# A two-layer model on one core: where bias weights are loaded, how means over partitions are taken, and the shape of the gated scores

## The chip, the cores and the metric

The kernel runs on one core of one Trainium2 chip. A core has TensorE (matrix products, called PE in the profile, with PEld for its weight loads), VectorE (DVE), ScalarE (ACT), GpSimd (POOL) and SyncE (SP), from whose queue all DMAs of this kernel are issued. The metric is the device time of one execution in microseconds.

## The reference, cut to what matters

The sequence has 2048 tokens of width 1024, everything is f32. Layer A is gated linear attention (4 heads, keys of 128, values of 256, chunks of 64 tokens), layer B is stick-breaking attention (16 heads of 64). Each is wrapped in an RMS norm, a modulation by a condition vector and a residual.

```
rms_norm(x) = x * rsqrt(mean(x*x over the width) + eps) * gain
shift, scale, gate = split(silu(c) @ w_ada + b_ada, 3)
h = rms_norm(x) * (1 + scale) + shift
# layer A, per head and chunk of 64 tokens, b = cumsum(log_sigmoid(gk)/16) in the chunk
scores = tril((q * exp(b)) @ (k * exp(-b)).T)
o = scores @ v + (q * exp(b)) @ state
state = exp(b_last) * state + (k * exp(b_last - b)).T @ v
x = x + gate * ((rms_norm(o) * silu(g)) @ w_out)
# layer B: k, v from hk = rms_norm(x)*(1+kv_scale)+kv_shift; q, g from h
# out = rms_norm(x + gate * (stick_breaking(q, k, v) * silu(g)) @ w_out, final_gain)
```

## The kernel before, in words

Activations lie transposed: the width is on the 128 partitions in 8 tiles (`KT`), and 512 tokens (`TG`) are the free dimension, so there are four groups of tokens (`NG`). A mean over the width is therefore a mean over partitions. `rstd` (L205) takes it on TensorE: the sum of squares over the 8 tiles, a [128x512] f32 tile, is multiplied by a 128x128 matrix of 1/1024 (`mean_d`) or 1/256 (`mean_v`), which leaves the mean on every partition; ScalarE and VectorE make the inverse root of it.

Most products are in three terms: a value is `hi`, rounded to fp32r by ScalarE, and `lo`, what is left, by VectorE (`split`, L221); `mm3` (L135) multiplies hi by hi, hi by lo and lo by hi. A product of plain f32 operands is in the trace as two matmul instructions.

`start` (L300) makes the first group's input: it loads x, starts the rows of the condition's weights (`ada_rows`, 16 tiles wa_l of 512 KB which VectorE multiplies into an accumulator aa_l), normalises x on GpSimd (L315), sums the accumulator over partitions (`ada_sum`, 16 matmul instructions for each half), and makes xn = x*a + b on VectorE, ScalarE and GpSimd (`scaled`, L327), then hi and lo of it. In this part the order of TensorE, ScalarE, VectorE and SP is that of the code.

`layer0` (L690) runs layer A group by group: value, key and query projections head by head (`qkv`), the gate (`gate`), the attention of a head (`gla`), the output gate and the output projection. `play` steps one main generator and beside it side generators with a delay and a stride, and so fixes TensorE's order; one yield of `mm3` is three matmuls. The order on the other engines is made by a planner from priorities (the order of the code, moved by `urgent` and `relaxed`) and its own estimate of times; at run time each engine takes its instructions in that fixed order. `gla` takes the scores of two chunks (128 keys by 128 queries) in one product (L466) and overwrites the corner where queries of the second chunk meet keys of the first by a 64 by 64 product with other key weights, `kn` (L467). After a head's output `po` come the squares (`ss_o`), five yields, and `rstd`. `normed_out` (L568) does the norm of a finished group (`ss_y`, `r_y`, x1n) as a side generator while the next group runs.

`bias_sums` (L655) runs in the third and fourth group: it loads the weights of layer B once (16 halves of 512 KB for each of two matrices, tiles wb), multiplies them by the shift on VectorE, and sums over partitions with two transposes and a reduction. Its tiles come from the pool `wraw` (3 buffers), as do the raw weights of every load (`load_half`, L104, DMA issued at L106) and later rows of the condition's weights. The pool `wsp` (10 buffers) holds hi and lo of two weight blocks, 4 buffers each; `m2` (22 buffers) holds [128x512] tiles.

Layer B (`layer1`) computes projections, scores, a scan and products with the values; its last stage `final` ends with an `rstd` per group and two half groups at the end.

Of the kernel before, what the change touches and what calls it, by code (L numbers as in the profile page):

```python
# [16 lines left out]
P = 128  # L17
# [17 lines left out]
def yoco_kernel(ctx: ExitStack, tc: tile.TileContext, I: dict, O: dict):  # L35
# [29 lines left out]
    def bank(pool, name):  # L65
# [7 lines left out]
    nc.gpsimd.memset(ident, 1.0)  # L73
    nc.gpsimd.affine_select(ident, ident, pattern=[[-1, P]], compare_op=ALU.is_equal,
                            fill=0.0, base=0, channel_multiplier=1)
    mean_d = cpool.tile([P, P], F32, tag="mean_d", name="mean_d")
    nc.vector.memset(mean_d, 1.0 / D)
    mean_v = cpool.tile([P, P], F32, tag="mean_v", name="mean_v")
    nc.vector.memset(mean_v, 1.0 / GV)
    ones = cpool.tile([P, 1], F32, tag="ones", name="ones")  # L80
    nc.vector.memset(ones, 1.0)
    epsc = cpool.tile([P, 1], F32, tag="epsc", name="epsc")
# [122 lines left out]
    def rstd(name, sq, mean, n=TG):  # L205


        ms = bank(po, f"ms_{name}")[:, 0:n]
        sq = sq if isinstance(sq, list) else [sq]
        for i, x in enumerate(sq):  # L210
            nc.tensor.matmul(ms, mean, x, start=i == 0, stop=i == len(sq) - 1)
        r = t2(f"r_{name}")[:, 0:n]
        q = t2(f"rq_{name}")[:, 0:n]
        nc.scalar.activation(r, ms, AF.Ln, bias=epsc)
        nc.scalar.activation(r, r, AF.Exp, scale=-0.5)
        nc.scalar.activation(q, r, AF.Square)
        nc.vector.scalar_tensor_tensor(q, ms, epsc, q, op0=ALU.add, op1=ALU.mult)
        nc.vector.scalar_tensor_tensor(r, q, -3.0, r, op0=ALU.add, op1=ALU.mult)
        return r
# [56 lines left out]

    def normed_in(T):

        r = rstd(f"x{T.g}", T.ss, mean_d)
        yield  # L280
        yield
        for i in range(4):
            xs = load_x(T.g, i, "xx")
            for j in range(2):
                modulate(T, 2 * i + j, xs[j], r)
                yield
# [13 lines left out]
    def start():  # L300

        T = start_group(0)
        w = I["w_ada"][0]
        rows = [ada_rows("l0", w, j, act) for j in range(2)]
        xs, sq = [], []
        for i in range(4):
            xs += load_x(0, i)
            for kt in (2 * i, 2 * i + 1):
                sq.append(t2(f"sq_x0_{kt}"))
                nc.scalar.activation(sq[kt], xs[kt], AF.Square)  # L310
        for _ in range(6):
            next(rows[0])
        r = rstd("x0", sq, mean_d)
        for kt in range(KT):
            nc.gpsimd.tensor_tensor(xs[kt], xs[kt], r, op=ALU.mult)  # L315
        accs = [result(g) for g in rows]
        gate_weights()
        ahead.append(next(blocks))
        cond = new_cond("l0", 2)
        pc = bank(po, "pc_l0")  # L320
        for j in range(2):
            ada_sum(pc[:, 8 * j:8 * j + 8], accs[j])
        nc.vector.tensor_tensor(cond, pc[:, 0:16], b_ada[:, 0:16], op=ALU.add)
        a, b = mods["l0m"] = modulation("l0", norm_gain[:, 0:8], cond)
        xn = [t2(f"xn_0_{kt}") for kt in range(KT)]

        def scaled(kt):  # L327
            s, t = a[:, kt:kt + 1], b[:, kt:kt + 1]
            if kt % 2 == 0 and kt:
                nc.scalar.activation(xn[kt], xs[kt], AF.Identity, bias=t, scale=s)  # L330
            else:
                eng = nc.vector if kt < 1 else nc.gpsimd
                eng.tensor_scalar(xn[kt], xs[kt], s, t, op0=ALU.mult, op1=ALU.add)

        scaled(0)
        for kt in range(KT):
            if kt + 1 < KT:
                scaled(kt + 1)
            h = new_h(0, kt)
            T.hs.append(split(h[:, 0], h[:, 1], xn[kt]))  # L340
        return T


# [38 lines left out]
    def gate(T, h):  # L382


        n = f"{T.g}_{h}"
        u = bank(po, f"u_{n}")
        nc.tensor.matmul(u, gk2[:, h * P:(h + 1) * P], T.lr[0:96], start=True, stop=True)
        bg = b_gk[:, h:h + 1]
        gk = t2(f"gk_{n}")
        e = t2(f"e_{n}")  # L390
        nc.vector.tensor_scalar(gk, u, bg, 0.0, op0=ALU.add, op1=ALU.min)
        nc.scalar.activation(e, u, AF.Abs, bias=bg)
        nc.scalar.activation(e, e, AF.Exp, scale=-1.0)
        nc.scalar.activation(e, e, AF.Ln, bias=1.0)
        nc.vector.tensor_tensor(gk, gk, e, op=ALU.subtract)
        b64 = e
        b128 = t2(f"b128_{n}")
        b64c = b64.rearrange("p (c t) -> p c t", t=64)
        b128c = b128.rearrange("p (c t) -> p c t", t=128)
        nc.vector.tensor_tensor_scan(b64, masks[:, 0], gk, 0.0, ALU.mult, ALU.add)  # L400
        nc.vector.tensor_tensor_scan(b128, masks[:, 1], gk, 0.0, ALU.mult, ALU.add)

        bl = m2.tile([P, 8], F32, tag="bl", name=f"bl_{n}", bufs=2)
        nc.vector.tensor_scalar(bl[:, 0:4], b128c[:, :, 127], 1.0 / GN, None, op0=ALU.mult)
        nc.vector.tensor_scalar(bl[:, 4:8], b64c[:, 0::2, 63], 1.0 / GN, None, op0=ALU.mult)
        G = Piece()
        G.ke, G.kf, G.kn, G.qe, G.qf = gk, t2(f"kf_{n}"), t2(f"kn_{n}"), b64, b128
        nc.scalar.activation(G.ke, b64, AF.Exp, scale=-1.0 / GN)
        for s in range(4):
            nc.scalar.activation(G.kf[:, s * P:(s + 1) * P], b128[:, s * P:(s + 1) * P], AF.Exp,  # L410
                                 bias=bl[:, s:s + 1], scale=-1.0 / GN)
            nc.scalar.activation(G.kn[:, s * 64:(s + 1) * 64], b64c[:, 2 * s, :], AF.Exp,
                                 bias=bl[:, 4 + s:5 + s], scale=-1.0 / GN)
        nc.scalar.activation(G.qe, b64, AF.Exp, scale=1.0 / GN)
        nc.scalar.activation(G.qf, b128, AF.Exp, scale=1.0 / GN)
        G.dec = m2.tile([P, 4], F32, tag="dec", name=f"dec_{n}", bufs=3)
        nc.scalar.activation(G.dec, bl[:, 0:4], AF.Exp)
        T.G[h] = G

    def qkv(T, h):  # L420
# [26 lines left out]
        yield from mm3(pk, wkq, 0, T.hs)  # L447
        with urgent():
            nc.vector.tensor_tensor(G.ke, pk, G.ke, op=ALU.mult)
            kn = G.kn[:, 0:256].rearrange("p (c t) -> p c t", t=64)  # L450
            nc.vector.tensor_tensor(kn, pk.rearrange("p (c t) -> p c t", t=64)[:, 0::2, :], kn, op=ALU.mult)
            nc.vector.tensor_tensor(G.kf, pk, G.kf, op=ALU.mult)
        pq = bank(pl, f"pq_{n}")
        yield from mm3(pq, wkq, 1, T.hs)
# [4 lines left out]
    def gla(T, h):  # L459
# [3 lines left out]
        psc = bank(pw, f"psc_{n}")  # L463
        for s in range(4):
            c0 = s * P
            nc.tensor.matmul(psc[:, c0:c0 + P], G.ke[:, c0:c0 + P], G.qe[:, c0:c0 + P], start=True, stop=True)  # L466
            nc.tensor.matmul(psc[0:64, c0 + 64:c0 + P], G.kn[:, s * 64:(s + 1) * 64],  # L467
                             G.qe[:, c0 + 64:c0 + P], start=True, stop=True)
            yield
        sc = t2(f"sc_{n}")  # L470
        with urgent():
# [42 lines left out]

        with urgent():
            ss = result(sumsq_steps(f"o{n}", pos))
        for _ in range(5):
            yield
        r = rstd(f"o{n}", ss, mean_v)
        on = t4(f"on_{n}", [P, 2, TG])  # L520
        for v2 in range(2):
            nc.vector.scalar_tensor_tensor(on[:, v2], pos[v2], o_gain[:, v2:v2 + 1], r,
# [45 lines left out]
    def normed_out(T):  # L568

        g = T.g  # L570
        ss = yield from sumsq_steps(f"y{g}", T.x1, 100)
        for _ in range(10):
            yield
        r = rstd(f"y{g}", ss, mean_d)
        for f in range(KT):
            nc.vector.tensor_tensor(T.x1[f], T.x1[f], r, op=ALU.mult)
            xn = tact(f"x1n_{g}_{f}")
            split(xn[:, 0], xn[:, 1], T.x1[f])
            nc.sync.dma_start(xn_d[g][:, f], xn.bitcast(F32))
            yield  # L580
# [74 lines left out]
    def bias_sums(i):  # L655
# [10 lines left out]
            nc.vector.tensor_reduce(biases[:, at:at + 2], pb.rearrange("p (j t) -> p j t", j=2),  # L666
                                    axis=mybir.AxisListType.X, op=ALU.add)

        before = None
        for p in range(SBP):  # L670
            acc = t2(f"bs_{i}_{p}")[:, 0:2 * P]
            for hf in range(2):
                raw = wraw.tile([P, 4, 256], F32, tag="wraw", name=f"wb_{i}_{p}_{hf}")
                nc.sync.dma_start(raw, I[which][p][:, 4 * hf:4 * hf + 4, :])
                for j in range(4):
                    kt = 4 * hf + j
                    s = b[:, kt:kt + 1]
                    with relaxed(200):
                        if kt == 0:
                            nc.vector.tensor_scalar(acc, raw[:, j], s, None, op0=ALU.mult)  # L680
                        else:
                            nc.vector.scalar_tensor_tensor(acc, raw[:, j], s, acc, op0=ALU.mult, op1=ALU.add)
                yield
            if before:
                total(*before)
            before = p, acc
        yield
        total(*before)

# [224 lines left out]
    def final(g, t0=0, n=TG):  # L914
# [8 lines left out]
        for fp in range(4):  # L923
# [9 lines left out]
            for j in range(2):  # L933
# [3 lines left out]
                                                   op0=ALU.mult, op1=ALU.add)  # L937
                x2s.append(x2[:, j])
                ss.add(x2[:, j])
        r = rstd(f"f{name}", ss.acc, mean_d, n)  # L940
        for f in range(KT):
            with relaxed(400):
                nc.vector.scalar_tensor_tensor(x2s[f], x2s[f], final_gain[:, f:f + 1], r,
# [182 lines left out]
```

## Time and profile before

| | us |
|---|---|
| median of 3 runs (lowest to highest) | 2676.28 (2675.8 to 2679.9) |
| the profiled execution, whole | 2677.76 |
| its span in the trace | 2676.1 |
| TensorE busy in the span | 2595.5 (97%) |
| VectorE busy | 2127.7 (80%) |
| ScalarE busy | 1519.0 (57%) |
| GpSimd busy | 171.4 (6%) |
| mean granted TensorE clock, as a share of full speed | 0.985 |

The trace is of one execution. A busy time counts instructions, and matmuls are pipelined, so the chain of waits gives the step from one matmul to the next better than the length of one instruction does. The span runs from the first to the last instruction; the 1.66 us between it and the whole lie outside the trace.

### The profile page before, as it was taken

The page shows a single profiled execution, that of the slowest core. Times are in us where ns is not written, and L with a number is a line of the kernel's source. Part 1 is how long each engine was busy: PE and PEld are TensorE (multiplying, and loading weights), DVE is VectorE, ACT ScalarE, POOL GpSimd, SP SyncE. Part 2 cuts the span into 40 slices and gives each one's busy share as a digit, 9 for nine tenths or more (in the row PEclk, how much of TensorE's full clock was granted, in tenths as well). Part 3 has the DMA queues.
Part 4 walks back from the last instruction along what each step waited for, and adds up shares of the span by engine and source line. Part 5 has one row for each costly group of instructions (what it writes and reads, how often), then busy time and mean ns, then how long its engine had stood idle before and what let it go on. Part 6 is the DMA issues. An engine that isn't in the chain of part 4 may idle for free.

```text
span 2676.1 us, 38236 instructions
## 1 busy us (share of the span) xinstructions
PE 2595.5 (97%) x14008; PEld 2184.6 (82%) x14008; DVE 2127.7 (80%) x2933; ACT 1519.0 (57%) x2677; POOL 171.4 (6%) x358
## 2 busy tenths in 40 slices
PE   5999999989998999999999999999999999999998
PEld 4888888878787887888888888888888888887887
DVE  7647667687867657987988978989889889889866
ACT  4746755564666435655655655556556556566644
POOL 3000000000000001001001010010010010010000
PEclk7999999989999999999999999999999999999999
DMA  6326345455744375424323333424233243413464
GB/s 248 118 72 212 126 163 184 157 197 173 252 157 160 133 245 207 168 75 150 110 103 123 120 133 104 153 79 170 83 138 119 77 148 111 146 64 123 151 213 144
DMA packets 121292, 388.70 MB, mean 145 GB/s; under 512 B 14384, under 2 KB 18608, under 8 KB 121104
## 3 DMA queue, kind: packets, MB, share of 16 engines
q1 hardware_dynamic: 121104, 386.25, 41.8%
q8 instruction: 111, 1.82, 0.3%
q14 instruction: 77, 0.63, 0.1%
HBM read 328.52 MB, written 40.89 MB: 138 GB/s over the span
## 4 chain that ended last, share of the span: by engine, by line
PE 82%; DVE 8%; ACT 5%; DMA 4%; issue 1%; SPq 0%; DVEq 0%; ACTq 0%
PE pt L862 9%; PE o L880 5%; PE z L846 5%; PE o L879 5%; PE z L845 5%; PE lq L142 2%; PE lk L142 2%; PE lg L142 2%; PE lk L143 2%; PE lk L144 2%; PE lg L143 2%; PE lq L143 2%; PE lg L144 2%; PE lq L144 2%; PE pf L142 2%; PE pf L143 2%
## 5 line engine op out<-in xcount | busy, mean ns | idle before, releaser
L865 ACT ACTIVATE sh<-pt 128x512 fp32r<-128x512 f32 (+3 forms) x640 | 340.4, 532 | 526.5 <-PE pt L862 516.6
L866 DVE SCALAR_TENSOR_TENSOR sl<-pt,sh 128x512 fp32r<-128x512 f32 (+3 forms) x640 | 384.9, 602 | 147.2 <-ACT sh L865 141.6
L854 DVE TENSOR_TENSOR_SCAN S<-S,S 128x512 f32<-128x512 f32 x384 | 490.1, 1276 | 9.0 <-ACT S L849 7.3
L862 PE MATMUL pt<-ident,S 128*128 128x128 f32 x2176 | 343.7, 273 | 7.2 <-DVE sl L866 7.2
L849 ACT ACTIVATE S<-z 128x512 f32<-128x512 f32 (+3 forms) x640 | 339.3, 530 | 14.8 <-PE o L880 5.8
L862 PEld LDWEIGHTS pt<-ident,S 128*128 128x128 f32 x2176 | 270.8, 140 | 81.6 <-DVE sl L866 13.1
L845 PE MATMUL z<-k,q 128*128 128x512 f32 (+3 forms) x640 | 283.3, 443 | 0.0
L880 PE MATMUL o<-sl,v 128*128 128x512 f32 (+3 forms) x640 | 233.7, 365 | 0.0
L846 PE MATMUL z<-k,ql 128*128 128x512 f32 (+3 forms) x640 | 233.3, 365 | 0.0
L879 PE MATMUL o<-sh,v 128*128 128x512 f32 (+3 forms) x640 | 230.2, 360 | 0.0
L854 DVE TENSOR_TENSOR_SCAN S<-S 128x128 f32<-128x128 f32 (+3 forms) x256 | 209.5, 821 | 17.3 <-POOL S L851 14.0
L851 POOL TENSOR_SCALAR_AFFINE_SELECT S<-S 128x128 f32<-128x128 f32 x256 | 86.7, 339 | 1228.3 <-ACT S L849 1228.3
L436 PE MATMUL pv<-wh_v,h 128*128 128x256 f32 x512 | 157.7, 308 | 0.0
L437 PE MATMUL pv<-wl_v,h 128*128 128x256 f32 x512 | 146.8, 287 | 0.0
L438 PE MATMUL pv<-wh_v,h 128*128 128x256 f32 x512 | 146.7, 286 | 0.0
L879 PEld LDWEIGHTS o<-sh,v 128*128 128x128 f32 x640 | 120.3, 188 | 28.4
L880 PEld LDWEIGHTS o<-sl,v 128*128 128x128 f32 x640 | 120.5, 188 | 26.5
L845 PEld LDWEIGHTS z<-k,q 128*128 128x128 f32 x640 | 121.7, 190 | 6.1
L846 PEld LDWEIGHTS z<-k,ql 128*128 128x128 f32 x640 | 123.2, 193 | 0.2
L142 PE MATMUL pg<-h,wh_g 128*128 128x512 f32 x256 | 112.7, 440 | 0.0
L142 PE MATMUL lv<-xb,wh_w_kv 128*128 128x512 f32 x256 | 104.6, 408 | 4.5 <-DVE g L823 3.1
L436 PEld LDWEIGHTS pv<-wh_v,h 128*128 128x128 f32 x512 | 99.9, 195 | 7.0 <-issue 2.8
(266 smaller groups left out, 6353.4 us busy)
## 6 DMA issues: line engine op xcount, KB each, us to landing
xb<-xn SPq DMA_DIRECT2D x256, 512.0 KB, 5.5
wa_l<-in_w_ada_dram SPq DMA_DIRECT2D x40, 512.0 KB, 5.0
wr_f<-in_w_out_dram SPq DMA_DIRECT2D x40, 512.0 KB, 4.2
x<-in_x_dram SPq DMA_DIRECT2D x32, 512.0 KB, 7.1
wr_v<-in_w_v_dram SPq DMA_DIRECT2D x32, 512.0 KB, 4.5
wr_kq<-in_w_kq_dram SPq DMA_DIRECT2D x32, 512.0 KB, 4.0
wr_g<-in_w_g_dram SPq DMA_DIRECT2D x32, 512.0 KB, 4.0
wr_out<-in_w_out_dram SPq DMA_DIRECT2D x32, 512.0 KB, 3.8
```

The costliest lines, as they stand in the source:

```text
L142: nc.tensor.matmul(out, hi, x[kt][0], start=first and i == 0, stop=False)
L143: nc.tensor.matmul(out, hi, x[kt][1], start=False, stop=False)
L436: nc.tensor.matmul(o, xh, hi, start=i == 0, stop=False)
L845: nc.tensor.matmul(z, L.q[:, h, tcol], k[:, h, 0:w], start=True, stop=False)
L846: nc.tensor.matmul(z, L.ql[h][:, tcol], k[:, h, 0:w], start=False, stop=True)
L849: nc.scalar.activation(s, z, AF.Sigmoid, scale=-SCALE_B)
L854: nc.vector.tensor_tensor_scan(s[:, ::-1], s[:, ::-1], s[:, ::-1], 1.0 if diag else self.before.S[tb][:, 0:1], ALU.mult, ALU.min)
L862: nc.tensor.transpose(pt[:, tb * P:(tb + 1) * P], self.S[tb][:, sb * P:(sb + 1) * P], ident)
L865: nc.scalar.activation(hi, pt[:, t0 * P:], AF.Copy, bias=-1.0)
L866: nc.vector.scalar_tensor_tensor(lo, pt[:, t0 * P:], -1.0, hi.bitcast(F32), op0=ALU.add, op1=ALU.subtract)
L879: nc.tensor.matmul(o, v, hi, start=self.diag and sb == 0, stop=False)
L880: nc.tensor.matmul(o, v, lo, start=False, stop=self.c == 0 and sb == 3)
```

## The change

Five edits. The matrices of 1/1024 and 1/256 are also kept in fp32r (`mean_r`), and `rstd` of a single tile splits that tile in hi and lo on ScalarE and VectorE and makes two fp32r products in place of one f32 product; in `gla` it comes seven yields after the squares and in `normed_out` 16 yields in all groups but the last (10 there). `start` leaves GpSimd out: VectorE makes x*a*r in one instruction, ScalarE adds b and rounds to hi, VectorE makes lo. The gated scores are two products of 128 keys by 64 queries; `kn` has 128 keys, those of the second chunk with the weights of `ke`, so `gate` makes one more exponential and `qkv` multiplies a whole tile. `bias_sums` takes its tiles from `wsp` and issues the next load right after the multiplications of the one before; the sums over partitions of one accumulator come one step after its last multiplication (three before).

```
-    mean_d = cpool.tile([P, P], F32, tag="mean_d", name="mean_d")
+    mean_d = t2("mean_d")[:, 0:P]
     nc.vector.memset(mean_d, 1.0 / D)
-    mean_v = cpool.tile([P, P], F32, tag="mean_v", name="mean_v")
-    nc.vector.memset(mean_v, 1.0 / GV)
+    mean_r = {}
+    for name, n in ("d", D), ("v", GV):
+        mean_r[name] = cpool.tile([P, P], F32R, tag=f"mean_{name}", name=f"mean_r{name}")
+        nc.scalar.activation(mean_r[name], mean_d, AF.Copy, scale=float(D / n))
...
 def rstd(name, sq, mean, n=TG):
-        sq = sq if isinstance(sq, list) else [sq]
-        for i, x in enumerate(sq):
-            nc.tensor.matmul(ms, mean, x, start=i == 0, stop=i == len(sq) - 1)
+        if isinstance(sq, list):
+            for i, x in enumerate(sq):
+                nc.tensor.matmul(ms, mean_d, x, start=i == 0, stop=i == len(sq) - 1)
+        else:
+            hi = t2(f"sh_{name}", F32R)[:, 0:n]
+            lo = t2(f"sl_{name}", F32R)[:, 0:n]
+            with urgent():
+                split(hi, lo, sq)
+            for i, x in enumerate((hi, lo)):
+                nc.tensor.matmul(ms, mean_r[mean], x, start=i == 0, stop=i == 1)
...
 def start():
-        for kt in range(KT):
-            nc.gpsimd.tensor_tensor(xs[kt], xs[kt], r, op=ALU.mult)
-        accs = [result(g) for g in rows]
-        gate_weights()
-        ahead.append(next(blocks))
-        cond = new_cond("l0", 2)
-        pc = bank(po, "pc_l0")
+        cond, pcs = new_cond("l0", 2), []
         for j in range(2):
-            ada_sum(pc[:, 8 * j:8 * j + 8], accs[j])
-        nc.vector.tensor_tensor(cond, pc[:, 0:16], b_ada[:, 0:16], op=ALU.add)
+            acc = result(rows[j])
+            if j:
+                gate_weights()
+                ahead.append(next(blocks))
+            pcs.append(bank(po, f"pc_l0_{j}"))
+            ada_sum(pcs[j], acc)
+        for j in range(2):
+            cols = slice(8 * j, 8 * j + 8)
+            nc.vector.tensor_tensor(cond[:, cols], pcs[j][:, 0:8], b_ada[:, cols], op=ALU.add)
         a, b = mods["l0m"] = modulation("l0", norm_gain[:, 0:8], cond)
         def scaled(kt):
-            s, t = a[:, kt:kt + 1], b[:, kt:kt + 1]
-            if kt % 2 == 0 and kt:
-                nc.scalar.activation(xn[kt], xs[kt], AF.Identity, bias=t, scale=s)
-            else:
-                eng = nc.vector if kt < 1 else nc.gpsimd
-                eng.tensor_scalar(xn[kt], xs[kt], s, t, op0=ALU.mult, op1=ALU.add)
+            h = new_h(0, kt)
+            xn = t2(f"xn_0_{kt}")
+            nc.vector.scalar_tensor_tensor(xn, xs[kt], a[:, kt:kt + 1], r, op0=ALU.mult, op1=ALU.mult)
+            nc.scalar.activation(h[:, 0], xn, AF.Identity, bias=b[:, kt:kt + 1])
+            return h, xn
...
+            h, xn = ready[kt]
+            nc.vector.scalar_tensor_tensor(h[:, 1], xn, b[:, kt:kt + 1], h[:, 0].bitcast(F32),
+                                           op0=ALU.add, op1=ALU.subtract)
...
 def gate(T, h):
-            nc.scalar.activation(G.kn[:, s * 64:(s + 1) * 64], b64c[:, 2 * s, :], AF.Exp,
+            nc.scalar.activation(G.kn[:, s * P:s * P + 64], b64c[:, 2 * s, :], AF.Exp,
                                  bias=bl[:, 4 + s:5 + s], scale=-1.0 / GN)
+        nc.scalar.activation(G.kn.rearrange("p (c t) -> p c t", t=P)[:, :, 64:], b64c[:, 1::2, :], AF.Exp,
+                             scale=-1.0 / GN)
...
 def qkv(T, h):
-            kn = G.kn[:, 0:256].rearrange("p (c t) -> p c t", t=64)
-            nc.vector.tensor_tensor(kn, pk.rearrange("p (c t) -> p c t", t=64)[:, 0::2, :], kn, op=ALU.mult)
+            nc.vector.tensor_tensor(G.kn, pk, G.kn, op=ALU.mult)
...
 def gla(T, h):
-            nc.tensor.matmul(psc[:, c0:c0 + P], G.ke[:, c0:c0 + P], G.qe[:, c0:c0 + P], start=True, stop=True)
-            nc.tensor.matmul(psc[0:64, c0 + 64:c0 + P], G.kn[:, s * 64:(s + 1) * 64],
-                             G.qe[:, c0 + 64:c0 + P], start=True, stop=True)
+            for at, k in (c0, G.ke), (c0 + 64, G.kn):
+                nc.tensor.matmul(psc[:, at:at + 64], k[:, c0:c0 + P], G.qe[:, at:at + 64], start=True, stop=True)
...
-        for _ in range(5):
+        for _ in range(7):
             yield
-        r = rstd(f"o{n}", ss, mean_v)
+        r = rstd(f"o{n}", ss, "v")
...
 def normed_out(T):
-        for _ in range(10):
-            yield
-        r = rstd(f"y{g}", ss, mean_d)
+        yield from pause(16 if g + 1 < NG else 10)
+        r = rstd(f"y{g}", ss, "d")
...
 def bias_sums(i):
+        def load(p, hf):
+            raw = wsp.tile([P, 4, 256], F32R, tag="wsp", name=f"wb_{i}_{p}_{hf}").bitcast(F32)
+            nc.sync.dma_start(raw, I[which][p][:, 4 * hf:4 * hf + 4, :])
+            return raw
+        seq = [(p, hf) for p in range(SBP) for hf in range(2)]
+        raw, before = load(*seq[0]), None
+        for n, (p, hf) in enumerate(seq):
+            yield
+            if hf == 0:
+                acc = t2(f"bs_{i}_{p}")[:, 0:2 * P]
+            with relaxed(200):
                 for j in range(4):
...
+            if hf == 0 and before:
+                total(*before)
+            before = p, acc
+            if n + 1 < len(seq):
+                raw = load(*seq[n + 1])
         yield
         total(*before)
```

## Rows read from the trace of the kernel before

**Rows 1.** The page, busy time of one engine with its share and instructions.
```profile
PE 2595.5 (97%) x14008; PEld 2184.6 (82%) x14008; DVE 2127.7 (80%) x2933; ACT 1519.0 (57%) x2677; POOL 171.4 (6%) x358
```

**Rows 2.** Busy time by engine in one stretch: stretch, length, engines, clock, DMA.
```profile
60.00:1050.00 990.00, 960.79 (x5268) 816.40 (x5266) 683.55 (x1020) 566.59 (x864) 21.52 (x34) 0.98 0.50 173
```

**Rows 3.** Who TensorE waited for, 57 to 1100 us: total, times, longest.
```profile
PE ms_o L211 <- DVE ss_o L196: 18.4, 4, 9.1
...
PE ms_y L211 <- DVE ss_y L196: 3.2, 1, 3.2
```

**Rows 4.** Busy time by engine in two stretches at half clock.
```profile
572.71:582.95 10.24, 5.40 (x18) 4.03 (x19) 6.25 (x10) 7.16 (x9) 0.00 (x0) 0.50 0.97 354
...
815.06:825.30 10.24, 4.22 (x13) 2.85 (x13) 7.02 (x12) 6.22 (x9) 0.00 (x0) 0.50 0.95 338
```

**Rows 5.** Busy time by engine around the first long wait.
```profile
555.00:577.00 22.00, 15.19 (x97) 13.52 (x95) 21.79 (x37) 13.11 (x25) 0.00 (x0) 0.90 0.67 240
```

**Rows 6.** The chain that ended last, 0 to 100 us: start, length, work.
```profile
20.87 1.29 DVE aa_l L236
...
40.62 3.59 PE pc_l L242 x16
...
57.20 0.23 PE plr L373
```

**Rows 7.** Instructions on tile wa_l, 0 to 60 us: ns min/median/max, starts.
```profile
L231 SPq DMA_DIRECT2D wa_l<-in_w_ada_dram x16: 327/328/689, 3.1 to 20.7; - x16
...
L236 DVE SCALAR_TENSOR_TENSOR aa_l<-wa_l,s_col,aa_l x14: 1276/1725/2174, 13.0 to 39.3; 128x1024 f32<-128x1024 f32 x14
...
DMA to landing us min/median/max: 8.5/10.2/11.0
```

**Rows 8.** Instructions in order of time, 0 to 60 us: start, length, engine.
```profile
21.10 17.07 POOL L315 TENSOR_TENSOR x<-x,r_x 128x512 f32<-128x512 f32 x8 [17.91 <-DVE r_x L218]
...
44.71 0.55 DVE L333 TENSOR_SCALAR xn<-x,a_l,cond_l 128x512 f32<-128x512 f32 x1
...
51.05 2.13 DVE L223 TENSOR_TENSOR h<-xn,h 128x512 fp32r<-128x512 f32 x3 [0.17 <-ACT h L222]
```

**Rows 9.** Groups by line, VectorE, 500 to 1000 us: busy, mean ns.
```profile
L223 DVE TENSOR_TENSOR og<-sg,og 128x512 fp32r<-128x512 f32 x16 | 10.7, 684 | 1.5 <-ACT og L222 1.4
```

**Rows 10.** The chain, 100 to 120 us.
```profile
111.48 0.86 PE ms_o L211 x2
...
113.06 0.22 PE psc L466 x2
...
113.28 0.26 PE psc L467 x2
...
113.53 0.32 PE pv L436
...
114.08 0.12 PE pv L436
```

**Rows 11.** Groups by line, ScalarE, 500 to 1000 us.
```profile
L222 ACT ACTIVATE og<-sg 128x512 fp32r<-128x512 f32 x16 | 10.0, 626 | 13.7 <-DVE sg L542 13.6
```

**Rows 12.** The chain, 150 to 154 us.
```profile
151.42 1.68 PE pc_g L242 x16
...
153.10 0.34 PE pg L142
```

**Rows 13.** Who the DMA queue of SP waited for, 500 to 1050 us.
```profile
SPq L106 <- DVE bs L682: 37.7, 18, 7.4
```

**Rows 14.** Instructions in order of time, 2660 to 2676 us.
```profile
2664.27 1.28 ACT L214 ACT_TABLE_LOAD   x1
...
2664.77 0.70 PE L211 MATMUL ms_f<-ss_f,mean_d 128*128 128x256 f32 x2 [1.48 <-DVE ss_f L196]
```

**Rows 15.** Instructions on tile wh_kq, 600 to 650 us.
```profile
L142 PE MATMUL pk<-h,wh_kq x8: 389/436/799, 640.6 to 646.6; 128*128 128x512 f32 x8
...
L117 DVE TENSOR_TENSOR wl_kq<-wr_kq,wh_kq x2: 1217/1222/1227, 614.9 to 625.1; 128x1024 fp32r<-128x1024 f32 x2
```

More of the change, by code (lines that the diff above doesn't have):

```diff
@@ L277, in normed_in @@
     def normed_in(T):
-        r = rstd(f"x{T.g}", T.ss, mean_d)
+        r = rstd(f"x{T.g}", T.ss, "d")
         yield
@@ L312, in start @@
             next(rows[0])
-        r = rstd("x0", sq, mean_d)
-        for kt in range(KT):
-            nc.gpsimd.tensor_tensor(xs[kt], xs[kt], r, op=ALU.mult)
-        accs = [result(g) for g in rows]
-        gate_weights()
-        ahead.append(next(blocks))
-        cond = new_cond("l0", 2)
-        pc = bank(po, "pc_l0")
-        for j in range(2):
-            ada_sum(pc[:, 8 * j:8 * j + 8], accs[j])
-        nc.vector.tensor_tensor(cond, pc[:, 0:16], b_ada[:, 0:16], op=ALU.add)
+        r = rstd("x0", sq, "d")
+        cond, pcs = new_cond("l0", 2), []
+        for j in range(2):
+            acc = result(rows[j])
[7 more added lines that the diff above has]
+            nc.vector.tensor_tensor(cond[:, cols], pcs[j][:, 0:8], b_ada[:, cols], op=ALU.add)
         a, b = mods["l0m"] = modulation("l0", norm_gain[:, 0:8], cond)
-        xn = [t2(f"xn_0_{kt}") for kt in range(KT)]
         def scaled(kt):
-            s, t = a[:, kt:kt + 1], b[:, kt:kt + 1]
-            if kt % 2 == 0 and kt:
-                nc.scalar.activation(xn[kt], xs[kt], AF.Identity, bias=t, scale=s)
-            else:
-                eng = nc.vector if kt < 1 else nc.gpsimd
-                eng.tensor_scalar(xn[kt], xs[kt], s, t, op0=ALU.mult, op1=ALU.add)
-        scaled(0)
+            h = new_h(0, kt)
[3 more added lines that the diff above has]
+            return h, xn
+        ready = [scaled(0)]
         for kt in range(KT):
             if kt + 1 < KT:
-                scaled(kt + 1)
-            h = new_h(0, kt)
-            T.hs.append(split(h[:, 0], h[:, 1], xn[kt]))
+                ready.append(scaled(kt + 1))
+            h, xn = ready[kt]
+            nc.vector.scalar_tensor_tensor(h[:, 1], xn, b[:, kt:kt + 1], h[:, 0].bitcast(F32),
+                                           op0=ALU.add, op1=ALU.subtract)
+            T.hs.append((h[:, 0], h[:, 1]))
         return T
@@ L667, in total @@
                                     axis=mybir.AxisListType.X, op=ALU.add)
[L669 to L674, printed above, removed]
+        def load(p, hf):
[9 more added lines that the diff above has]
+            with relaxed(200):
                 for j in range(4):
@@ L677, in bias_sums @@
                     s = b[:, kt:kt + 1]
[L678 to L684, printed above, removed]
+                    if kt == 0:
+                        nc.vector.tensor_scalar(acc, raw[:, j], s, None, op0=ALU.mult)
+                    else:
+                        nc.vector.scalar_tensor_tensor(acc, raw[:, j], s, acc, op0=ALU.mult, op1=ALU.add)
+            if hf == 0 and before:
                 total(*before)
             before = p, acc
+            if n + 1 < len(seq):
+                raw = load(*seq[n + 1])
         yield
@@ L939, in final @@
                 ss.add(x2[:, j])
-        r = rstd(f"f{name}", ss.acc, mean_d, n)
+        r = rstd(f"f{name}", ss.acc, "d", n)
         for f in range(KT):
```

## The prediction

> **What bounds the kernel now.** I read the page first: TensorE is busy 97% of the span [rows 1], so a gain must be TensorE time taken away or a gap of TensorE closed. Then the stretches: from 60 to 1050 us, layer A's groups, TensorE is busy 960.8 of 990 us and VectorE 683.6 [rows 2]; layer B's bulk is not edited, so all but the start and the end is decided here. Then who TensorE waited for: ms_o for the sum of squares four times, 18.4 us, and ms_y once, 3.2 us [rows 3]. After the two longest waits the granted clock is 0.50, its 1.2 GHz level, for 10.24 us each, in which TensorE works 5.40 and 4.22 us [rows 4]; at the full level that work takes half, so the clock costs 4.8 us more. The reader is to see what stands behind the first of them: VectorE is busy 21.79 of 22 us up to its end [rows 5], with the norm of the group before (L576, L223), bias products and the condition's rows in one queue, and ScalarE, in order, reaches the squares of po late. Last the chain from 0 to 60 us, which runs through VectorE's aa_l, then ada_sum on TensorE, then the first tiles of h [rows 6].
>
> **The start.** Row products take 1.28 us undisturbed and 2.17 at most [rows 7]; the long ones lie inside GpSimd's 17.07 us of L315 [rows 8]. From 20.87 us to the start of ada_sum at 40.62 [rows 6] VectorE does ten of them (two of the first row, eight of the second). Without GpSimd that is 10 x 1.31 with their gaps = 13.1 us, end 34.0. The loads allow it: the last wa_l is issued at 20.7 and lands 8.5 to 11.0 us later [rows 7], by 31.7 at worst, and the last product starts at 32.7. So ada_sum (3.59) ends at 37.6 and the first xn starts at 38.1 where it was 44.71 [rows 8]: 6.6 us earlier. Then some is given back. VectorE now makes both xn and lo, 16 instructions at the 0.684 us of a two-tensor instruction of that size [rows 9] and gaps, 11.5 us, so lo of the last tile is there at 49.6; before it was at 53.2 (51.05 + 2.13, [rows 8]). TensorE was then behind by 4.2 us (its last plr ends at 57.43, [rows 6]); a tile is two plr of 0.23 [rows 6] and six pv of 0.12 [rows 10], 1.2 us, less than the 1.44 in which VectorE makes one, so it would end about 1.2 us after the last lo, at 50.8: 6.6 us gained. Behind by 4.2 again it gains 3.6. At the half clock all through, a tile takes it 2.4 us, eight 19, and from 38.8 on it ends at 57.7: nothing. I take -5.5, range 0 to -6.6. Behind it TensorE is busy 97% of the time [rows 2], so the shift is kept.
>
> **The means.** An f32 mean costs the chain 0.86 us for two matmuls [rows 10]; a 512-column fp32r matmul is one step of 0.23 (the plr of [rows 6]), so hi and lo cost 0.46. Layer A has 23 of these (16 for heads, 4 for y, 3 for x): 23 x 0.40 = -9.2 us, and TensorE is the bound there, so it counts. The split adds ScalarE 0.63 [rows 11] and VectorE 0.68 [rows 9] each, some 30 us on the two, beside TensorE: VectorE would stand at 0.71 of layer A instead of 0.69. As latency it is 1.3 us in front of each mean; two more yields in gla are six matmuls of 0.23, 1.4 us, which covers it for a head if the queues are short. If they are long, as in [rows 5], the split stands behind what is queued; that is in the next term but one.
>
> **The scores.** One pair now costs 0.22 + 0.26 and makes the pv after it 0.32 where a pv is 0.12 [rows 10]: 0.68 us. The new pair is four matmuls, each with a full weight load and 64 columns. The trace has no such matmul; the nearest row is ada_sum, full weights and one column: 1.68 us for 16, 0.105 each, and the matmul behind it 0.34 instead of 0.23 [rows 12]. Two passes of 64 columns are half the 0.11 that a 128-column f32 instruction takes (0.22 for two), so the weight load should set the step. 4 x 0.105 + 0.11 = 0.53, 0.15 less; 64 pairs give -9.6 us. Bounds: with the 0.13 of each L467 as step and its exit of 0.20 it is 0.72, +2.6 us; with no exit cost 0.42, -16.6 us. I take the value by the ada_sum row. The Trainium skill, "TensorEngine Tiling (Array Packing)", section "Key Properties", says that changing the tiling mode drains TensorE; by that rule the exit belongs to the 64-wide weights that go, and the sum would be -16.6. The ada_sum row has an exit of 0.11 with no 64-wide weights, so I do not use it but as a rival. The wider kn adds per head one exponential of 256 columns on ScalarE and half an instruction (0.34 us) on VectorE, 16 times, off the path.
>
> **Waits in layer A.** Three edits bear on the 18.4 + 3.2 us of waits and 4.8 us of clock. The mean of y comes six steps of its generator later, each every second yield, 12 x 0.69 = 8.3 us, against a wait of 3.2 and a split of 1.3: that wait goes, -3.2. Its flood of x1n work moves too, by about as much, so that at the squares of head 0 only some of its 8 tiles stand in the queues. The bias tiles leave wraw: raw weight loads waited 37.7 us in 18 cases for a bias product to free a buffer [rows 13], and ScalarE, in order, waits for those loads; and a bias product no longer follows its own load at once. But VectorE's amount of work does not fall, the flood still meets head 0, and the split needs VectorE too. I take half of 18.4 + 4.8: -11.6. Bounds: all of it (-23.2), or +10 (a wait as long as the longest, 9.1 us, once more). Together -14.8.
>
> **The bias sums' own steps.** 32 loads, products and pairs of transposes stay as many. The transposes come one step of 12 yields (8.3 us) after the last product of their accumulator instead of three; four relaxed products must fit before them. Cost 0, to +3.
>
> **The end.** Five means of the last stage get the split with no added steps. At the very end ScalarE loads its table right behind the last square and the mean starts at 2664.77 [rows 14]; the copy goes in front of both. Half-width copy and subtraction are below 0.63 and 0.68: +0.9 us on the last chain. Of the other four, two already made TensorE wait (the last of them 1.48, [rows 14]): 2 x 1.3 = +2.6. Saved 3 x 0.40 + 2 x 0.20 = -1.6. Sum +1.9.
>
> **Sum.** -5.5 - 9.2 - 9.6 - 14.8 + 1.9 = -37.2 us. The profiled execution took 2677.76 and the median is 1.5 lower: 2677.8 - 37.2 - 1.5 = 2639 us.
>
> **Rivals.** (1) The waits stay: VectorE is as full around head 0 as now, and the means wait as long, only at other places. For it: [rows 5], and that the planner's fixed order is made anew. Against: [rows 13], and the 8.3 us of y. -37.2 + 14.8 = -22.4, 2654 us. (2) The whole exit cost of the scores goes: 7 us better, 2632. For it: an exit of 0.20 after L467 against 0.11 after ada_sum. The tiling rule named above says the same. (3) Slower: the bias tiles take the two buffers that wsp has to spare, so the next weight block's hi and lo begin only when the block before has left TensorE. The price is a TensorE wait for the second half's copy and subtraction, some 1.2 (a copy of 1024 columns by the 626 ns for 512, [rows 11]) + 1.22 [rows 15] = 2.4 us, at each of 32 blocks in the two last groups, 77 us: 2677.8 - 37.2 - 1.5 + 77 = 2716. It decides from 1.2 us a block on. Against: the key weights are split by 626.3 and first used at 640.6 [rows 15], 14 us of margin. (4) No change: new waits of VectorE, loaded by another 35 us, and an unwarmed start eat the gain, 2676.
>
> **How the numbers follow.** Forecast 0.50 (its own range 2625 to 2650), rival 1 0.24, rival 2 0.12, rival 3 0.08, rival 4 0.06. The range 2619 to 2664 leaves out rivals 3 and 4 and the far ends of the unknown terms, some 0.2. A measurement of this kernel can tell 0.2%, 5 us, from no change: faster 0.86, same 0.05, slower 0.09.
>
> **What would show it.** Right: aa_l products all near 1.3 us and the first xn near 38 us; ms steps of 0.23; psc pairs near 0.43 to 0.53 with their exit; no wait of ms_y, and waits of ms_o under 12 us in all; the last chain some 1 us longer. Wrong: psc steps above 0.15 each; waits of TensorE for wl or wh tiles; new stretches at the half clock in the groups; ScalarE's split late behind x1n.

## The result, and the profile after

The changed kernel takes 2703.5 us (median of 4 runs, 2701.2 to 2706.0) against 2676.0 before: ratio 1.0098, 95% interval 1.0086 to 1.011. It is slower by 26 us by this ratio (27.5 by the medians), where 2639 with a range of 2619 to 2664 was forecast. The profiled execution took 2702.52 us, its span is 2700.7.

The trace shows where along the span the time goes. The first matmul on h (`plr`) starts at 40.6 us, 5.4 earlier than before. The first output projection (`py`) starts at 217.93 where it was 225.95, 8.0 earlier. The first matmul of layer B (`lv`) starts at 998.55 where it was 981.12, 17.4 later. From there to the end it is 1702.1 us against 1695.0. So the start gained, the first group gained, and the three groups after it lost 25.4 us; the part from there on lost some 7. The busy rows of the stretch from the first py to the first lv (start and end, length, then TensorE, its weight loads, VectorE, ScalarE, GpSimd, clock, DMA), of before:

```profile
225.95:981.12 755.17, 730.43 (x4001) 620.49 (x4000) 543.15 (x819) 433.27 (x654) 9.55 (x12) 0.98 0.52 178
```

and of after, with the stretch around one long wait below it:

```profile
217.93:998.55 780.62, 725.69 (x4002) 624.64 (x4000) 558.86 (x838) 451.81 (x689) 8.71 (x12) 0.97 0.51 174
...
572.00:585.30 13.30, 2.89 (x25) 2.69 (x23) 13.30 (x23) 5.95 (x11) 0.00 (x0) 0.80 0.71 280
```

Both rows hold 4000 matmuls with their weight loads. TensorE was idle 755.17 - 730.43 = 24.7 us before and 54.9 after, 30.2 more. The time in it at the half clock (summed over the steps of matmuls that start in stretches of clock 0.50) rose from 20.0 to 39.5 us, and half of these 19.5 us, 9.8, is time lost, if the same work takes half as long at the full level (a plain `pv` steps 0.21 us at the half clock and 0.12 at the full one). Against that stand 48 score pairs at 0.23 less (11.0) and 18 means at 0.40 less (7.2). 30.2 + 9.8 - 18.2 = 21.8 of the 25.4; the other 3.6 are not assigned here. Who TensorE waited for, 57 to 1100 us (total, times, longest), which answers [rows 3]:

```profile
PE ms_o L221 <- ACT sh_o L232: 23.8, 6, 10.4
PE pb L675 <- DVE bs L698: 16.0, 3, 6.1
PE ms_x L221 <- ACT sh_x L232: 6.0, 3, 2.1
...
PE ms_y L221 <- ACT sh_y L232: 3.3, 1, 3.3
PE ms_x L221 <- DVE sl_x L233: 2.0, 3, 0.9
...
PE ms_o L221 <- DVE sl_o L233: 1.4, 4, 0.4
```

The sum of squares is no longer what a mean waits for: its hi and lo are (`sh` and `sl`). The longest wait, 10.43 us before the mean of the third group's first head, is seen on ScalarE and VectorE in order of time (start, length, work; idle before in brackets). ScalarE:

```profile
575.96 1.83 ACT L232 ACTIVATE x1n<-x 128x512 fp32r<-128x512 f32 x3 [3.98 <-DVE x L587]
...
579.58 1.83 ACT L232 ACTIVATE x1n<-x 128x512 fp32r<-128x512 f32 x3 [1.29 <-DVE x L587]
583.19 0.63 ACT L232 ACTIVATE x1n<-x 128x512 fp32r<-128x512 f32 x1 [1.78 <-DVE x L587]
584.12 0.63 ACT L232 ACTIVATE x1n<-x 128x512 fp32r<-128x512 f32 x1 [0.30 <-DVE x L587]
584.66 0.61 ACT L232 ACTIVATE sh_o<-ss_o 128x512 fp32r<-128x512 f32 x1
```

VectorE:

```profile
574.64 0.68 DVE L199 TENSOR_TENSOR ss_o<-ss_o,sq_o 128x512 f32<-128x512 f32 x1
575.25 1.89 DVE L587 TENSOR_TENSOR x<-x,r_y 128x512 f32<-128x512 f32 x3
...
585.47 0.68 DVE L233 TENSOR_TENSOR sl_o<-ss_o,sh_o 128x512 fp32r<-128x512 f32 x1
```

The sum ss_o is ready at 575.3. The copy sh_o, 0.61 us of work, runs at 584.66: ahead of it on ScalarE stand eight x1n copies of the group that is done, and these wait for VectorE, which is busy 13.30 of 13.30 us there. In the trace before, in the stretch of [rows 5], the squares themselves stood behind the last of the same eight copies on ScalarE:

```profile
573.89 0.63 ACT L222 ACTIVATE x1n<-x 128x512 fp32r<-128x512 f32 x1 [1.50 <-DVE x L576]
574.42 0.58 ACT L192 ACTIVATE ss_o<-po 128x512 f32<-128x512 f32 x1
```

Now the sum comes in front of them and the split behind.

### The profile page after: what moved, and what is told of

Its sections match the earlier page's. It is cut to its first block, busy times and chain, and to the rows that moved or that the text cites. A ratio compares the mean times of both kernels' runs of the same rounds, so it can differ in the third digit from the quotient of the medians.

```text
span 2700.7 us, 38340 instructions
## 1 busy us (share of the span) xinstructions
PE 2590.0 (96%) x14008; PEld 2191.1 (81%) x14008; DVE 2147.3 (80%) x2968; ACT 1545.3 (57%) x2725; POOL 146.7 (5%) x346
## 4 chain that ended last, share of the span: by engine, by line
PE 60%; DVE 3%; DMA 1%; ACT 0%; issue 0%; DVEq 0%; SPq 0%; ACTq 0%
PE pt L879 9%; PE o L897 5%; PE z L863 5%; PE o L896 4%; PE z L862 4%; PE lk L145 2%; PE lq L145 2%; PE lk L146 2%; PE lg L145 2%; PE lk L147 2%; PE lq L146 2%; PE lq L147 2%; PE lg L146 2%; PE lg L147 2%; PE lv L145 2%; PE pf L145 2%
## 5 line engine op out<-in xcount | busy, mean ns | idle before, releaser
L866 ACT ACTIVATE S<-z 128x512 f32<-128x512 f32 (+3 forms) x640 | 339.5, 531 | 14.5 <-PE o L897 5.6
L871 DVE TENSOR_TENSOR_SCAN S<-S 128x128 f32<-128x128 f32 (+3 forms) x256 | 209.6, 821 | 18.3 <-POOL S L868 15.1
L145 PE MATMUL lg<-xb,wh_w_qg 128*128 128x512 f32 x256 | 104.6, 409 | 0.0
```

Of the source, the lines that this page charges most:

```text
L145: nc.tensor.matmul(out, hi, x[kt][0], start=first and i == 0, stop=False)
L866: nc.scalar.activation(s, z, AF.Sigmoid, scale=-SCALE_B)
L871: nc.vector.tensor_tensor_scan(s[:, ::-1], s[:, ::-1], s[:, ::-1], 1.0 if diag else self.before.S[tb][:, 0:1], ALU.mult, ALU.min)
```

## The experiments

Three theories were held against each other. A, place: the split stands in the two queues where its mean is written, not where its sum is ready, behind other work. B, load: VectorE and ScalarE have no room for the added work, wherever it stands. C, pauses: seven and sixteen yields push other work into a worse place. The kernel before gave medians of 2677 to 2679 us beside these runs.

**Each edit alone.** Only the hunks named were taken from the change.

> Only the gated scores are changed (two products of 64 queries, the wider kn). Theory: in the changed kernel a pair takes 0.45 us of TensorE with its exit where it took 0.68, so 64 pairs give -14.7 us and nothing else moves: about 2661. Rival (the added work of ScalarE and VectorE loads two engines that are behind, whatever their order): less than half of it arrives, 2669 or more.

Measured 2672.4, ratio 0.9977 (0.9968 to 0.9986): the number of the rival, less than half of the 14.7 us.

> Only the first group's input is changed (no GpSimd). Theory: the first plr comes 5.4 us earlier and the first py about 6, and the shift is kept: 2669 to 2671. Rival: later weights are not there earlier, so the shift is lost by the end of the first group: 2676.

Measured 2671.9, 0.9976 (0.9966 to 0.9985), 1 us above the range of the theory.

> Only the means are changed (hi and lo in fp32r, 7 and 16 yields). Theory: -9.2 us of matmuls, against new waits for the split: 8 us at the three means of x, which got no more steps, some 4 in the last stage, and at head 0 of the third and fourth group 3 to 6 us each, since the planned order has one or two x1n copies ahead of the split: 2676 to 2684. Rival: the split's work alone is the loss, and it shows at every head: 2690.

Measured 2707.3, 1.0111 (1.0093 to 1.0128), far above the range of the theory, and above the rival's 2690.

> Only the bias sums are changed (loads in wsp one step ahead, transposes one step after their products). Theory: three waits of transposes for late products, some 16 us, and their stretches at half clock: 2688 to 2700, though the squares of head 0 now stand ahead of three of the eight x1n copies. Rival (the wsp buffers make weights late): waits of TensorE for wl or wh tiles, and none for bs.

Measured 2679.4, 1.0005 (0.9996 to 1.0014): no loss, where 2688 to 2700 was expected. By these ratios the four alone are -6.1, -6.5, +29.6 and +1.3 us, together +18.3; the whole change is +26. The means are the loss. The scores gain 0.23 a pair, 14.7 us for 64, but TensorE now comes earlier to a VectorE that is no earlier: in the kernel with the scores alone it waited 14.0 us for ss_y and 13.9 for ss_o, 27.9 together against 21.6 [rows 3]. In the kernel with the bias loads alone the old waits have moved to the transposes:

```profile
PE pb L664 <- DVE bs L687: 20.6, 5, 8.3
...
PE ms_o L211 <- DVE ss_o L196: 1.3, 2, 1.1
```

**The place of the split, and the pauses.** In the first kernel the means edit stays alone, but hi and lo are made when the sum of squares is finished. The cut shows a head; the sums of x and y get the same line:

```
         with urgent():
             ss = result(sumsq_steps(f"o{n}", pos))
+        ss = presplit(f"o{n}", ss)
         for _ in range(7):
             yield
```

> The means edit alone, with the split of the sum of squares into hi and lo written where the sum is finished, not where the mean is taken. Theory A (place: the split is late because it is issued together with its mean, behind ScalarE's and VectorE's other work): the waits of TensorE for ms_o, ms_x and ms_y, 25 us in the means edit alone, fall under 10 us and the time to 2668-2680. Theory B (load: VectorE and ScalarE have no room for 35 us more): 2700 or more wherever the split stands, the waits only move. Theory C (the longer pauses shift the other work into each other): 2695 or more, with waits for on, pb and psc rather than for sh.

Measured 2677.5, 0.9996 (0.9987 to 1.0006): 30 us better than the same means with the split at the mean, and in the range of theory A. The waits for ms fell from 25.2 us to 11.3, not quite under the 10 expected. The mean of x in the second group shows it. With the split at the mean, the sum is ready on VectorE at 216.70:

```profile
216.01 0.69 DVE L199 TENSOR_TENSOR ss_x<-ss_x,sq_x 128x512 f32<-128x512 f32 x1
```

and ScalarE makes hi 15 us later, after other work that ends with a load of its function table and a gate, so that TensorE waits:

```profile
230.03 1.28 ACT L544 ACT_TABLE_LOAD   x1
231.32 0.60 ACT L544 ACTIVATE sg<-pg 128x512 f32<-128x512 f32 x1
231.81 0.62 ACT L232 ACTIVATE sh_x<-ss_x 128x512 fp32r<-128x512 f32 x1
```

With the split at the sum, ScalarE makes hi as soon as the sum ends at 213.96, and the mean at 226 waits for nothing:

```profile
214.00 0.63 ACT L236 ACTIVATE sh_x<-ss_x 128x512 fp32r<-128x512 f32 x1 [0.72 <-DVE ss_x L199]
```

The busy rows of the stretch from py to lv, split at the mean:

```profile
228.14:1005.92 777.78, 741.24 (x4002) 626.63 (x4001) 556.96 (x838) 448.62 (x677) 9.84 (x12) 0.97 0.52 174
```

and at the sum:

```profile
224.01:972.58 748.57, 725.79 (x4002) 619.62 (x4001) 557.34 (x837) 448.08 (x676) 9.22 (x12) 0.99 0.53 181
```

VectorE and ScalarE do the same work, 557 and 448 us, in 29 us less. In this pair theory A holds for the bulk of the loss, and B alone, which asked for 2700 or more, falls. The pauses alone, with f32 means:

> The kernel before with only the longer pauses (7 yields before the mean of a head, 16 before that of y) and its f32 means. Theory A and B: no split, so 2670-2679 (the wait of ms_y goes, ms_o's stay or shrink). Theory C: most of the loss is here, 2695 or more.

Measured 2684.0, 1.0025 (1.0016 to 1.0035), between the ranges. TensorE waited 9.3 us for `on` (the normed output of a head, which reads the banks of po) before the next `po`, which is not among the waits of before: the banks of po come free two yields later. C is a part, some 6 us, and no more. Beside these pauses the means with the split at the sum do gain: 2677.5 against 2684.0.

**The bias sums in company.** The transposes of an accumulator go back to three steps after its last product, once in the whole change and once with the split at the sum besides:

```
-            if hf == 0 and before:
-                total(*before)
-            before = p, acc
+            if hf == 0 and len(done) == 2:
+                total(*done.pop(0))
+            if hf == 1:
+                done.append((p, acc))
```

> The whole change, only the transposes of a bias accumulator three steps after its last product as before, not one. If the 16 us for pb are a cost of their own: 2683-2692 (2703 less those waits and their half clock). If the lateness of VectorE behind them only shows at the next mean instead: 2697-2706, with the pb waits gone and those of ms larger by as much.

Measured 2703.4, 1.0097 (1.0079 to 1.0116): the second expectation. The waits for bs fell from 16.0 to 4.0 us and those of ms_y, hi and lo together, rose from 3.3 to 12.4. Where TensorE meets the late engine is a matter of place; the lateness stays.

> The whole change, with the split written where the sum of squares is finished, and with the transposes of a bias accumulator three steps after its last product as before, not one. Theory A: 2645-2665, waits of ms under 10 us and of pb under 3. Theory B: 2690 or more. Theory C: 2680-2700.

Measured 2687.4, 1.0042 (1.0029 to 1.0055), 16 us better by the split's place, but outside the ranges of theories A and B and inside that of C. Waits for on (13.6 us), bs (7.8) and sc (7.0) came where most of those for hi went; those for on are the ones that the pauses alone brought.

> The whole change without the bias loads. If the bias edit costs as little in company as alone (+1): 2698-2704, and the means' place is all of the loss. If it is a good part of the loss in company (the pb waits, wsp shared with the weights): 2682-2692.

Measured 2699.2, 1.0079 (1.0064 to 1.0094): the first expectation, 4 us under the whole change.

> The whole change without the bias loads, the split written where the sum of squares is finished. Theory A (only the split's place cost): scores, start and these means add to 2658-2670. If the bias edit was not what kept the kernel with the same split at 2687: 2678-2690, with waits for on and sc before po as there.

Measured 2674.5, 0.9996 (0.9986 to 1.0006), a miss, between the two ranges: scores, start and these means together only reach the time of the kernel before. So these means, pauses included, still cost some 6 us in this company, since scores and start alone are faster:

> The scores edit and the start edit together, without the means and the bias loads. If the two gains (-6.1 and -6.5 us alone) are independent: 2664 (2659-2670). If a gain of TensorE here only arrives earlier at waits for VectorE: 2670-2676.

Measured 2668.8, 0.9967 (0.9956 to 0.9979): of 12.6 us alone 9 are left together, at the upper end of the range for independent gains. The split's place is worth 2699.2 - 2674.5 = 24.7 us without the bias loads and 2703.4 - 2687.4 = 16.0 with them; the bias loads cost 4 us in company of the late split and 13 in company of the early one, although alone they cost 1.

> As the kernel with the split at the sum and without the bias loads, but with the pauses of before (5 and 10 yields). If the longer pauses cost by freeing po's banks later (the pauses alone were +6.5 us, with 9.3 us of waits for on): 4 to 10 us faster than with the long pauses, 2650-2662. If their cover of the split is worth more: 3 to 10 us slower, with waits for sh_o and sl_o above 15 us.

Measured 2679.0, 1.0005 (0.9996 to 1.0015): the cover is worth more than the earlier banks, 16.7 us of waits for sh_o and 14.5 for sh_y.

**Load against order.** In two kernels six of the eight products of each bias accumulator are left out (`for j in range(1)`); in the stretch from py to lv that takes 42 us off VectorE (560 to 518 with the late split). The loads stay.

> The change without the bias loads, the split where the mean is taken as in the change, and six of eight bias products left out. If the split's place costs by itself: 2688-2697, a little under the 2699 with all products, with waits for sh_o, sh_y, sh_x as there. If VectorE's sum of work makes it late: 2660-2676.

Measured 2681.3, 1.0018 (1.0009 to 1.0027): 18 us less than with all products, and between the two ranges.

> As the kernel with the split at the sum and without the bias loads, but six of the eight products of each bias accumulator on VectorE are left out (the loads stay), some 45 us of VectorE in the third and fourth group. If VectorE's sum of work decides: the waits of these two groups (some 20 us) go, those of the second group (6.4 us before po) stay: 2648-2660. If order decides: 2668-2678.

Measured 2669.4, 0.9971 (0.9961 to 0.9981): 5 us less, in the range for order. Place costs 24.7 us with the products and 11.8 without them, so half of what the late split costs here depends on VectorE's load: it is the dearer, the fuller the queue it stands in. With the split at the sum the same load costs 5 us.

The next kernels change the order of the eight x1n steps:

```
         for f in range(KT):
-            nc.vector.tensor_tensor(T.x1[f], T.x1[f], r, op=ALU.mult)
-            xn = tact(f"x1n_{g}_{f}")
-            split(xn[:, 0], xn[:, 1], T.x1[f])
+            with relaxed(300 if g + 1 < NG else 0):
+                nc.vector.tensor_tensor(T.x1[f], T.x1[f], r, op=ALU.mult)
+                xn = tact(f"x1n_{g}_{f}")
+                split(xn[:, 0], xn[:, 1], T.x1[f])
```

> Scores and start edits, the mean of y six steps later as in the change, and the eight x1n steps of a finished group put behind (priority lowered by 300), so that they no longer stand ahead of the squares of the next group's first head. If these steps ahead of the squares are what TensorE waits for at ms_o and ms_y (28.8 us in the two edits alone): 2650-2662, waits of ms_o and ms_y under 12. If VectorE's sum of work there decides: 2665-2672, the waits at other tiles.

Measured 2658.0, 0.9925 (0.991 to 0.994), the time expected if these steps are the cause, and faster than both kernels. The waits of ms_y are gone; those of ms_o are 17.5 us, not under 12. The later mean without this edit:

> Scores and start edits and the mean of y six steps later, the x1n steps at their priority of before. If the later mean alone takes away the wait of ms_y (14.3 us in the two edits alone) and the x1n steps then stand no worse before the squares: 2656-2663. If the x1n steps just move onto the squares and the gain came from putting them behind: 2665-2672.

Measured 2669.4, 0.9973 (0.9963 to 0.9983): the second expectation, no gain over scores and start. The wait of ms_y is gone, and one of 18.4 us for ss_o has come, since all eight x1n copies stand ahead of the squares in the third group. On ScalarE:

```profile
570.15 1.23 ACT L222 ACTIVATE x1n<-x 128x512 fp32r<-128x512 f32 x2 [1.78 <-DVE x L577]
571.28 0.58 ACT L192 ACTIVATE ss_o<-po 128x512 f32<-128x512 f32 x1
```

Then the same order of the x1n steps beside the hi and lo means:

> The change without the bias loads, the split written at the sum, heads' means five yields after the squares as before, and the x1n steps put behind. If order decides: 2650-2662, waits for on, sc, sh under 15 us in layer A (35 with the longer pause and the x1n steps in place). If VectorE's sum of work decides: 2668-2680.

Measured 2669.5, 0.9968 (0.9959 to 0.9978), in the range for VectorE's sum of work and not in that for order. This kernel differs from the one with 2658.0 by the hi and lo means alone, split at the sum: they cost 11.5 us although each takes 0.40 us less of TensorE. Its longest wait, 6.76 us before `po` at 542, shows how. ScalarE:

```profile
534.90 0.57 ACT L459 ACTIVATE v<-pv 128x512 f32<-128x512 f32 x1
540.33 0.63 ACT L236 ACTIVATE sh_y<-ss_y 128x512 fp32r<-128x512 f32 x1 [4.86 <-DVE ss_y L199]
540.87 0.58 ACT L488 ACTIVATE sc<-psc 128x512 f32<-128x512 f32 x1
```

The copy of the scores was ready to go, but the urgent split stands ahead of it in the fixed order and waits 4.86 us for its own sum. GpSimd masks the scores behind it, and `po` needs them. TensorE's waits for `sc` are 13.9 us in this kernel and 1.1 in the one with 2658.0, and the three over 1 us (4.36, 6.76 and 1.91) all have sh_y ahead of `sc` on ScalarE; in the two longer ones sh_y waits 1.62 and 4.86 us for its sum. So order is seen in the trace where the time alone spoke for load; what the 11 us of added VectorE work in the stretch from py to lv cost by themselves was not separated.

**The mean of y after that of the head.** One edit on the fastest kernel so far: `pause(26 ...)`.

> As the fastest so far (scores, start, x1n steps behind, 2658), with the mean of y 26 steps after its squares: it is then taken after the mean of the first head, so the chain of r_y on ScalarE no longer stands ahead of that head's squares (552 to 556 us in the trace of the fastest so far). If that chain is what the first head's mean waits for (5.4, 6.0 and 5.1 us): 2645-2654. If the wait goes to the second head or to po instead: 2656-2664.

Measured 2650.0 (2646.2 to 2651.0), 0.9899 (0.9883 to 0.9914): the fastest of all, 27 us under before and 53 under the change. The three largest of its waits of TensorE, 57 to 1100 us:

```profile
PE ms_o L211 <- DVE ss_o L196: 7.8, 5, 2.3
PE lv L142 <- DMA xb<-xn: 3.5, 3, 3.0
PE po L495 <- POOL sc L476: 3.3, 3, 2.1
```

and its stretch from py to lv:

```profile
218.18:951.08 732.90, 715.66 (x4002) 613.91 (x4000) 545.83 (x819) 435.30 (x666) 10.95 (x12) 1.00 0.55 183
```

TensorE is idle 17.2 us in it (24.7 before, 54.9 after) and at the half clock 6.8 us (20.0 and 39.5). VectorE's work is 545.8 us, no less than the 543.2 of the kernel before. Against scores and start alone (2668.8) only the order differs, so 19 of the 27 us are order; the rest came with those two edits.

Why the planner puts a split beside its mean though it is marked urgent was not run: that its two tiles get their buffers of `m2` at that point of the code is argued only.

## Why the prediction was wrong, step by step

**The start: right in the main.** Forecast -5.5, the first plr is 5.4 earlier and the edit alone is -6.5. The first xn starts at 38.21 where 38.1 was forecast. The last plr is 4.0 earlier, since VectorE ends the last lo at 52.6 and not at 49.6. The first plr before and after:

```profile
45.97 0.64 PE L372 MATMUL plr<-h,lrw 128*32 128x512 f32 x1 [1.78 <-ACT h L222]
...
40.64 0.63 PE L383 MATMUL plr<-h,lrw 128*32 128x512 f32 x1 [3.91 <-ACT h L341]
```

**The steps of the means and scores: right, the scores' gain taken too small.** A mean is two steps of 0.23 as forecast. A score pair with its exit takes 77.41 - 76.84 - 0.12 = 0.45 us, where 0.53 was taken and 0.68 stood before [rows 10]: 64 x 0.23 = 14.7 us, not 9.6. The answer to the psc rows of [rows 10]:

```profile
76.72 0.28 PE L451 MATMUL pv<-wh_v,h 128*128 128x256 f32 x1
76.84 0.33 PE L480 MATMUL psc<-e,gk 128*128 128x64 f32 x2
77.01 0.39 PE L480 MATMUL psc<-e,kn 128*128 128x64 f32 x2
77.21 0.36 PE L449 MATMUL pv<-wh_v,h 128*128 128x256 f32 x1
77.41 0.28 PE L450 MATMUL pv<-wl_v,h 128*128 128x256 f32 x1
...
107.80 0.40 PE L221 MATMUL ms_o<-sh_o,mean_rv 128*128 128x512 f32 x1
108.03 0.40 PE L221 MATMUL ms_o<-sl_o,mean_rv 128*128 128x512 f32 x1
108.27 0.28 PE L449 MATMUL pv<-wh_v,h 128*128 128x256 f32 x1
```

The exit fell from 0.20 to 0.08 us. The Trainium skill, "TensorEngine Tiling (Array Packing)", "Key Properties", says that changing the tiling mode drains TensorE. Most of the exit, 0.12 of 0.20 us, did go with the 64-wide weights, so the trace agrees in the main, though no run here shows a drain as such.

**The split's cover: the step that failed.** The prediction called the added VectorE and ScalarE work "beside TensorE" and said of its latency that two more yields, 1.4 us, cover it "for a head if the queues are short. If they are long, as in [rows 5], the split stands behind what is queued; that is in the next term but one." In that term it got one clause, "and the split needs VectorE too", and no price. The 1.3 us of the split are its length, not its lateness: in the means edit alone hi of x was made 15 us after its sum was ready, and three means of x, which never waited before, each waited some 2.0 us for hi and 0.7 for lo. So -9.2 came out as +29.6 alone, and 30 of that went away when only the split's place was changed.

**The waits in layer A: the sign was wrong.** Forecast -14.8, bounds -23.2 to +10. The idle time of TensorE rose by 30.2 us and the half clock cost 9.8 more. The bias term's "0, to +3" hid 16.0 us of waits for bs, which by the run with late transposes are lateness met at another place and not a cost of the transposes. The term "that wait goes, -3.2" for ms_y holds in the run with scores, start and the later mean, but the x1n steps moved onto the head's squares, which the prediction expected to be only "some of its 8 tiles".

**The end: mis-sized.** Forecast +1.9. From the first lv to the end it is 7.1 us longer. Waits for ms_f rose from 2.5 to 6.1 us, and matmuls at the half clock took 15.8 us there where it was 8.8, some 3.5 lost. The last mean waits 1.93 and its second product runs at the half clock:

```profile
2688.97 0.38 PE L221 MATMUL ms_f<-sh_f,mean_rd 128*128 128x256 f32 x1 [1.93 <-ACT sh_f L232]
2689.43 0.58 PE L221 MATMUL ms_f<-sl_f,mean_rd 128*128 128x256 f32 x1
```

**The rivals.** Rival 1 (the waits stay) was nearest in kind; they grew instead. Rival 2's mechanism (the exit goes) is mostly right. Rival 3, the slower one, is refuted as a mechanism: in layer A of the change and of the bias edit alone TensorE has no wait for a wl or wh tile. Rival 4 named new waits of a fuller VectorE, but took them to eat the gain and no more. The slower rival that was missing is the split's place: 23 splits in fixed queues, each as late as what stands ahead of it. In company that place is worth 16 us with the bias loads and 25 without them; what else makes up the 26 us of the whole change (bias loads, pauses, fuller queues) was not split further, as these terms do not add.

## What to carry to other kernels

When a change takes time from the bounding engine by giving work to others, price the place of that work in their in-order queues, not its length: list what stands ahead of it, and when its own input is there. Issue it when its input is ready, but not ahead of work that others wait for, since an urgent instruction whose input is late holds up all behind it. Where waits only change their name from run to run, look for the block of work ahead of them that nobody needs soon, here the x1n steps, and move that.

## What the hardware showed beyond that

A wait of TensorE costs more than its length here. In the trace after, TensorE was idle from 574.9 to 585.3 us ahead of a mean, and the granted clock was at its 1.2 GHz level from 579.9 to 590.1. The second product of that mean steps 0.59 us where an undisturbed one steps 0.23; the first steps 0.89, but it is followed by a wait for lo, which is done at 586.15:

```profile
579.90:590.10 10.20, 4.69 (x18) 4.08 (x19) 9.56 (x19) 7.60 (x11) 0.00 (x0) 0.50 0.90 358
```

Short waits can cost clock as well: in the means edit alone the two waits of 2.15 and 0.68 us before the products of ms_x at 232.5 and 233.7 were followed by 3.4 us at 0.50. With the split at the sum, where this mean waits for nothing, the clock is 1.00 from 224 to 240. The kernel with the means edit alone had 36.5 us of idle time between py and lv, 12 more than before, and 40.2 us at the half clock where before had 20.0.
